# Gate columns of two chunks as one 2x2 block product in seven products; conditioning sums in other stages

## The chip, the cores and the metric

One core of one Trainium2 chip. The metric is device time in microseconds of one execution of the program, inputs in HBM to outputs in HBM; the median of three runs is given.

## What is computed

Two layers of a gated trunk, for 640 tokens: 512 latent tokens and 128 context tokens, with the same weights and separate conditioning. Cut to what matters:

```python
# per layer; x (640, 1024)
shift, scale, gate = split(silu(cond) @ w_mod[l] + b_mod[l], 3)
h = layernorm(x) * (1 + scale) + shift
q, k, v, z_a, cb, cc, cx, z_b, fx, z_c, g = split(h @ w_in[l])      # g: 3 x 1024 columns
y_a = attention(q, k, v) * silu(z_a)
y_b = cb * dwconv3(cc * cx) * silu(z_b)
y_c = real_dft2(fx) * silu(z_c)
gates = sigmoid(g.reshape(-1, 3, 1024))
merged = sum(gates[:, b] * (y[b] @ w_branch[l][b]) for b in range(3))
x = layernorm(alpha * x + gate * (merged @ w_o[l])) * ln_g[l] + ln_b[l]
```

## The kernel before

Activations lie transposed, channels on the partitions. `act` (line 115) is [128, 5 token tiles, 2, 8, 128]: 1024 channels as 8 blocks k of 128, 640 tokens, and each number as a high and a low part in the reduced format fp32r (`split`, line 80: ScalarE copies to the short format, VectorE subtracts to get the rest). A product of two such numbers takes three matmuls: high x high, low x high, high x low.

`inproj` (466) computes one chunk of 128 columns of h @ w_in for all tokens. Its weights are two units of 4 k-blocks, 128x512 (256 KB) each. `product` (457) runs over k and over two token groups of 256 and 384 columns, three matmuls each, into a two-bank PSUM tile from a pool of two (`pm`). `branch` (478) does the same with 4 k-blocks and the transposed branch outputs yb, yc or ya as the moving operand.

Of the 58 chunks of w_in, 24 are gate columns (`C_G` on). In the merge (lines 887 to 904) each chunk of branches 1 (yb) and 2 (yc) is followed by the branch product of the same output columns; for branch 0 (ya) all eight gate chunks come first and then all eight products. `use_g` (829) takes the sigmoid out of PSUM on ScalarE; `use_p` (840) multiplies by it out of PSUM and adds to `mg` on VectorE, and splits the finished sum into `act`, from which the output projection reads.

```python
for k in range(nk):
    for t0, t1, a, b in GROUPS:                      # columns 256:512 and 512:896
        mh, ml = moving(k, 0, t0, t1), moving(k, 1, t0, t1)
        nc.tensor.matmul(ps[:, a:b], lhsT=ld.w(0, k), rhs=mh, ...)
        nc.tensor.matmul(ps[:, a:b], lhsT=ld.w(0, k), rhs=ml, ...)
        nc.tensor.matmul(ps[:, a:b], lhsT=ld.w(1, k), rhs=mh, ...)
```

**Order of the work.** The program is a list of jobs in a fixed order (`run`, 163). Weight loads are issued ahead on the SP queue through a ring of `N_RAW` = 4 raw tiles, and split through a ring of `N_HL` = 5 tiles. Within this, a scheduler (`schedule_with_timeline_sim`, 1114) sets each engine's order of instructions when the program is built; it prefers what stands earlier in the list. On the chip each engine takes its own list in that order, and waits. Large tiles live in storage tags A to F and act, one buffer each; a tile of the same tag gets the buffer only when every reader and writer of the earlier tile is done. Before the change A holds Q, then yc, then the gates `ga` of branch 0; B holds K and V, then mg; C ya; D yb; E the softmax tile P, then the DFT matrix; F the gates of ya.

**Conditioning.** `w_mod` is 6 groups of 512 columns per layer; of the 12 the first four are done at the start on TensorE. The other eight are done on VectorE as sums over 8 k-blocks with a scalar per partition (`mod_add`, 198: lines 201 and 204), followed by a transpose, a reduction and one small matmul (`mod_sum`, 207). All eight groups are 32 pieces of two k-blocks, which the merge of layer 0 puts between its chunks (`piece`, 883).

**Other stages.** Attention (584 to 730) is ten units of a token tile and a key head per layer, scores two units ahead of values, with input products (`fills`) between them. The Fourier part (733 to 875) follows with four groups of channels, then the merge, then the output projection (943), whose `load_wo` (857) splits four large tiles of w_o into tags E, D, F and A.

Of the kernel before, what the change touches and what calls it, by code (L numbers as in the profile page):

```python
# [9 lines left out]
F32 = mybir.dt.float32  # L10
# [8 lines left out]
NT = 5  # L19
# [4 lines left out]
N_RAW = 4  # L24
# [10 lines left out]
def body(nc, tc, I, O, ctx):  # L35
# [8 lines left out]
    tq = pool("tq", 3)  # L44
# [80 lines left out]
    class Unit:  # L125
        def __init__(self, src, nm, plain):
            self.src, self.nm, self.plain = src, nm, plain
            self.read = self.used = False
            self.stage = build_stage[0]

        def dma(self):
            self.raw = wr.tile([128, 512], F32, name=f"raw{self.nm}", tag="raw")
            nc.sync.dma_start(out=self.raw, in_=self.src)

        def split(self, eng):
            self.hl = wp.tile([128, 2, 512], F32R, name=f"hl{self.nm}", tag="hl")
            copy(self.hl[:, 0], self.raw)
            eng.tensor_tensor(out=self.hl[:, 1], in0=self.raw, in1=fr(self.hl[:, 0]), op=ALU.subtract)  # L138
            self.read = True

    class Load:
        def __init__(self, src, n, nm, plain=False):
            self.units = [Unit(src[:, i * 512:(i + 1) * 512], f"{nm}_{i}", plain) for i in range(n)]

        def raw(self, i):
            return self.units[i].raw

        def w(self, z, k):
            return self.units[k // 4].hl[:, z, (k % 4) * 128:(k % 4 + 1) * 128]

# [12 lines left out]
    def run():  # L163
        units = [u for ld, _ in jobs if ld for u in ld.units]
        parts = [u for u in units if not u.plain]
        loaded = halved = 0
        for i, (ld, bd) in enumerate(jobs):
            while i >= 3:
                if (loaded < len(units) and units[loaded].stage <= stage[0]
                        and (loaded < N_RAW or i > 3 and units[loaded - N_RAW].read)):  # L170
                    units[loaded].dma()
                    loaded += 1
                elif (halved < len(parts) and hasattr(parts[halved], "raw")
                      and (halved < N_HL or parts[halved - N_HL].used)):
                    behind = () if halved == 4 or halved > 7 else ("xT",) if halved < 4 else ("hi", "lo")
                    with ExitStack() as st:
                        for name in behind:
                            st.enter_context(tc.issue_after(last[name].ins))
                        parts[halved].split(nc.gpsimd if halved < 4 or parts[halved].nm in POOL_UNITS else nc.vector)
                    halved += 1  # L180
                else:
                    break
            if ld:
                bd(ld)
                for u in ld.units:
                    u.read = u.used = True
# [35 lines left out]

    mod_raw = {}
# [242 lines left out]
    def inproj(l, c, use):  # L466
        ld = Load(I["w_in"][l, c], 2, f"w{l}_{c}")
# [10 lines left out]
    def branch(l, b, c, y, use):  # L478
        def body(ld):
            use(product(mmt(f"pb{l}_{b}_{c}"), ld, 4, lambda k, i, t0, t1: y()[:, k, i, t0 * 128:t1 * 128]))  # L480
        job(body, Load(I["w_branch"][l, b, c], 1, f"b{l}_{b}_{c}"))
# [7 lines left out]
    def layer(l):  # L489
        S = {}  # L490

# [10 lines left out]
        def begin():  # L502
# [14 lines left out]
            S["P"] = big.tile([128, 2, 4, 512], F32, name=f"P{l}", tag="E")  # L517
# [202 lines left out]

        job(scores(0))
# [107 lines left out]
        def use_g(b, c):  # L829
            def use(ps):  # L830
                if b == 0:
                    if c == 0:
                        S["ga"] = big.tile([128, NK, TOK], F32, name=f"ga{l}", tag="A")
                    nc.scalar.activation(S["ga"][:, c], ps, AF.Sigmoid)
                else:
                    S["sg"] = row(f"gs{l}{b}{c}")
                    nc.scalar.activation(S["sg"][:, :TOK], ps, AF.Sigmoid)  # L837
            return use

        def use_p(b, c):  # L840
            def use(ps):
                if b == 1 and c == 0:
                    S["mg"] = big.tile([128, NK, TOK], F32, name=f"mg{l}", tag="B")
                mg = S["mg"][:, c]
                if b == 1:
                    mul(mg, ps, S["sg"][:, :TOK])
                    return
                sg = S["sg"][:, :TOK] if b == 2 else S["ga"][:, c]
# [8 lines left out]
        def load_wo(i, tg, q):  # L857
            def body(ld):
                if q == 0:
                    flat = tg in "EF"  # L860
# [5 lines left out]
            job(body, Load(I["w_o"][l, i // 2, (i % 2) * 2 + q], 2, f"o{l}{i}{q}", True))  # L866

        inproj(l, C_FX, use_fx(0))
        inproj(l, C_FX + 1, use_fx(1))
        for g in range(4):  # L870
            job(channels(g))
            inproj(l, C_ZC + g, use_zc(g))
            job(positions(g))
# [252 lines left out]
```

## Time and profile before

| | |
|---|---|
| median of three runs | 1288.0 us (1287.6 to 1288.98) |
| profiled execution, span | 1287.4 us |
| TensorE busy | 1262.0 us, 8304 matmuls |
| VectorE, ScalarE, GpSimd busy | 779.7, 497.4, 172.4 us |
| HBM read | 124.19 MB |

The profile is one execution; its span runs from the first to the last instruction, and the median of the runs is 0.6 us above it. PE is TensorE's matmuls, PEld its weight loads, DVE VectorE, ACT ScalarE, POOL GpSimd and SP the queue that issues most loads. Matmuls are pipelined: one shows a duration longer than the distance to the next, so the distance between starts is what one costs.

### The profile page before, as it was taken

Reading aid. Unit: us, or ns where it says so; the run is one execution under the profiler, and the core shown is the slowest. Engines: PE = TensorE matmul, PEld = TensorE weight load, DVE = VectorE, ACT = ScalarE, POOL = GpSimd, SP = SyncE. Lnnn points to the kernel's source line nnn. Section 1 sums busy time; section 2 is a strip of 40 time slices with the busy share of each in tenths; the row PEclk is TensorE's granted clock in tenths of the full one; section 3 lists DMA queues with packets and bytes.
Section 4 is the critical chain, followed back from the end, with each engine's and each line's share of the span. In section 5 each row is a group of like instructions: output and inputs, shape, how many; then the busy total and the mean of one; then the engine's idle time right before and its main releaser. Section 6 shows DMA issues by size and latency. Waiting matters only on the chain.

```text
span 1287.4 us, 20922 instructions
## 1 busy us (share of the span) xinstructions
PE 1262.0 (98%) x8304; PEld 1218.7 (95%) x8304; DVE 779.7 (61%) x1418; ACT 497.4 (39%) x929; POOL 172.4 (13%) x164
## 2 busy tenths in 40 slices
PE   5999999999999999999999999999999999999997
PEld 3799999999999999999789999999999999999986
DVE  6785566664599999326887665666455323321576
ACT  5546556543432322222345646555344222222210
POOL 3303323210000000000230234232000000000001
PEclk9999999999999999999999999999999999999999
DMA  9322111131265655221612111113113223222141
GB/s 379 98 78 67 65 51 58 58 115 59 75 223 180 211 179 174 74 74 54 233 71 78 64 61 58 50 58 114 68 56 117 91 91 91 74 75 74 50 180 49
DMA packets 58761, 131.07 MB, mean 102 GB/s; under 512 B 6888, under 2 KB 7464, under 8 KB 58408
## 3 DMA queue, kind: packets, MB, share of 16 engines
q1 hardware_dynamic: 57504, 125.35, 29.2%
q0 software_dynamic: 720, 4.10, 0.9%
q8 instruction: 65, 1.06, 0.4%
q10 hardware_dynamic: 440, 0.30, 0.1%
q14 instruction: 32, 0.26, 0.1%
HBM read 124.19 MB, written 5.52 MB: 101 GB/s over the span
## 4 chain that ended last, share of the span: by engine, by line
PE 95%; DVE 3%; issue 1%; DMA 0%; POOL 0%; ACT 0%; SPq 0%; DVEq 0%; POOLq 0%; ACTq 0%
PE p L461 21%; PE p L463 21%; PE p L462 20%; PE pb L461 4%; PE pb L463 4%; PE pb L462 4%; PE o L951 3%; PE o L950 3%; PE o L949 3%; PE pt L647 2%; PE s L598 2%; PE p L347 2%; PE po L652 1%; PE po L653 1%; PE modp L407 1%
## 5 line engine op out<-in xcount | busy, mean ns | idle before, releaser
L461 PE MATMUL p<-act,hlw 128*128 128x256 f32 (+1 forms) x1792 | 562.4, 314 | 0.9 <-ACT vt L69 0.9
L463 PE MATMUL p<-act,hlw 128*128 128x256 f32 (+1 forms) x1792 | 556.3, 310 | 0.0
L462 PE MATMUL p<-act,hlw 128*128 128x256 f32 (+1 forms) x1792 | 554.6, 309 | 0.0
L461 PEld LDWEIGHTS p<-act,hlw 128*128 128x128 f32 x1792 | 338.4, 189 | 2.9 <-ACT vt L69 1.2
L462 PEld LDWEIGHTS p<-act,hlw 128*128 128x128 f32 x1792 | 337.2, 188 | 1.3
L463 PEld LDWEIGHTS p<-act,hlw 128*128 128x128 f32 x1792 | 337.4, 188 | 1.0
L138 DVE TENSOR_TENSOR hlw<-raww,hlw 128x512 fp32r<-128x512 f32 x226 | 159.2, 706 | 188.1 <-ACT hlw L69 185.3
L69 ACT ACTIVATE hlw<-raww 128x512 fp32r<-128x512 f32 x232 | 145.3, 629 | 247.8 <-PE p L463 163.9
L629 POOL TENSOR_SCALAR P<-P,rc 128x384 f32<-128x384 f32 (+2 forms) x80 | 111.9, 1413 | 232.8 <-ACT hlw L69 103.0
L204 DVE SCALAR_TENSOR_TENSOR moda<-rawm,scond,moda 128x512 f32<-128x512 f32 x112 | 79.2, 748 | 2.3 <-DMA rawm<-in_w_mod 2.2
L138 DVE TENSOR_TENSOR hlb<-rawb,hlb 128x512 fp32r<-128x512 f32 x48 | 33.1, 689 | 57.3 <-ACT hlb L69 57.2
L69 ACT ACTIVATE hlb<-rawb 128x512 fp32r<-128x512 f32 x48 | 30.3, 632 | 87.1 <-PE p L463 79.8
L950 PE MATMUL o<-wo,act 128*128 128x512 f32 (+1 forms) x168 | 63.7, 379 | 0.0
L949 PE MATMUL o<-wo,act 128*128 128x512 f32 (+1 forms) x168 | 63.7, 381 | 0.0
L951 PE MATMUL o<-wo,act 128*128 128x512 f32 (+1 forms) x168 | 62.9, 379 | 0.0
L257 POOL TENSOR_TENSOR rso<-rso,nhalf 128x1 f32<-128x1 f32 x10 | 13.7, 1374 | 334.0 <-DVE rso L256 334.0
L837 ACT ACTIVATE gs<-p 128x640 f32<-128x640 f32 x32 | 22.6, 705 | 91.0 <-PE p L463 91.0
L72 DVE TENSOR_TENSOR pT<-pt,pT 128x512 fp32r<-128x512 f32 x60 | 40.0, 688 | 23.2 <-ACT pT L69 23.1
L138 POOL TENSOR_TENSOR hlw<-raww,hlw 128x512 fp32r<-128x512 f32 x6 | 9.4, 1586 | 294.0 <-DVE mvo L254 288.4
L69 ACT ACTIVATE pT<-pt 128x512 fp32r<-128x512 f32 x60 | 35.0, 594 | 34.8 <-PE pt L647 26.5
L601 DVE CUSTOM_DVE_ANT_0 P<-s,mask 128x384 f32<-128x384 f32 (+1 forms) x64 | 38.6, 620 | 8.4 <-PE s L598 8.2
L623 ACT ACTIVATE P<-P,nm 128x384 f32<-128x384 f32 (+1 forms) x64 | 42.1, 658 | 1.8 <-DVE es L72 1.4
(221 smaller groups left out, 1909.6 us busy)
## 6 DMA issues: line engine op xcount, KB each, us to landing
raww<-in_w_in SPq DMA_DIRECT2D x232, 256.0 KB, 2.7
rawm<-in_w_mod SPq DMA_DIRECT2D x48, 512.0 KB, 4.3
rawb<-in_w_branch SPq DMA_DIRECT2D x48, 256.0 KB, 2.7
rawo<-in_w_o SPq DMA_DIRECT2D x32, 256.0 KB, 2.7
dft<-in_dft POOLq DMA_DIRECT2D x2, 1542.0 KB, 8.4
x<-in_x SPq DMA_DIRECT2D x5, 512.0 KB, 6.0
xr<-in_x SPq DMA_DIRECT2D x5, 512.0 KB, 8.4
xs<-xr SPq DMA_DIRECT2D x5, 512.0 KB, 2.9
```

Of the source, the lines that this page charges most:

```text
L69: nc.scalar.activation(out, in_, AF.Copy)
L72: nc.vector.tensor_tensor(out=out, in0=a, in1=b, op=ALU.subtract)
L138: eng.tensor_tensor(out=self.hl[:, 1], in0=self.raw, in1=fr(self.hl[:, 0]), op=ALU.subtract)
L204: nc.vector.scalar_tensor_tensor(out=acc[:, c], in0=w, scalar=scond[:, k, c:c + 1], in1=acc[:, c], op0=ALU.mult, op1=ALU.add)
L461: nc.tensor.matmul(ps[:, a:b], lhsT=ld.w(0, k), rhs=mh, start=k == 0, stop=False)
L462: nc.tensor.matmul(ps[:, a:b], lhsT=ld.w(0, k), rhs=ml, start=False, stop=False)
L463: nc.tensor.matmul(ps[:, a:b], lhsT=ld.w(1, k), rhs=mh, start=False, stop=k == nk - 1)
L623: nc.scalar.activation(P[:, g, :W], srcs[g], AF.Exp, scale=0.125, bias=nm_[:, g:g + 1], accum_out=sm[:, g:g + 1])
L629: nc.gpsimd.tensor_scalar(out=P[:, g, :W], in0=P[:, g, :W], scalar1=rc[:, g:g + 1], scalar2=None, op0=ALU.mult)
L949: nc.tensor.matmul(ps, lhsT=act[:, t, 0, k], rhs=w[:, 0], start=k == 0, stop=False)
L950: nc.tensor.matmul(ps, lhsT=act[:, t, 0, k], rhs=w[:, 1], start=False, stop=False)
L951: nc.tensor.matmul(ps, lhsT=act[:, t, 1, k], rhs=w[:, 0], start=False, stop=k == NK - 1)
```

## The change

Two chunks of gate columns are taken as the rows of a 2x2 block matrix (a11, a12; a21, a22): the chunks m and m+1 down, the two halves of k across. The activations are the other one: the halves of k down, and two halves of the tokens across (the first and the last 64 of each tile of 128, 320 columns each). The four blocks of the result are made from seven products of 4 k-blocks and 320 columns instead of eight (Strassen's scheme). For that VectorE forms four sums of weight tiles per pair, and once per layer four sums of the activations: three in tiles `T` of their own, and the fourth written over a block of `act`. Four of the seven products accumulate in one bank "y", two in "z", one in "x"; copies and additions take the partial sums into the gate tiles between them. The branch products of a pair now stand between the products of the following pair; for branch 0 they still come after all gates, but the first pair of branch 0 holds the last two products of yc.

The conditioning groups are spread: three to the attention stage of layer 0, one to its Fourier stage, two to its merge and two to the merge of layer 1. mg and xr move to tag E, w_o's tiles to D, B, F and A; the ring of raw tiles has 6 buffers, the pool of 643-column rows 5 instead of 3; the ring for descriptors of POOL's loads is set to 2048 bytes. The loading code becomes a list of steps (splits and sums) in place of units.

```diff
-N_RAW = 4
+N_RAW = 6
-    tq = pool("tq", 3)
+    tq = pool("tq", 5)
...
+    class Sum:
+        def __init__(self, out, a, b, frees=()):
+            self.raws, self.frees = [out, a, b], frees
+
+        def emit(self, eng):
+            out, a, b = self.raws
+            sub(out.tile, a.tile, b.tile)
...
+    def mod_steps(groups, acc, raws):
...
+                fetch(i + len(raws()) - 1)
+                mod_add(acc(), k, raws()[i % len(raws())])
+                if k == NK - 1:
+                    mod_sum(l, n, acc())
...
+        side = mod_steps(((0, 4), (0, 5), (1, 0)) if l == 0 else (), lambda: S["moda"], lambda: S["modr"])
...
             job(values(u))
+            beside(1)
             if u + 2 < 10:
                 job(scores(u + 2))
-                fills(2)
+                fills(1)
+                beside(1)
+                fills(1)
+                beside(1)
...
+        def sums(q):
+            def body():
+                def put(i, t):
+                    hi, lo = (S["T"][i][:, z, 2 * q:2 * q + 2].rearrange("p k n -> p (k n)") for z in range(2))
+                    split(hi, lo, t[:, :TOK])
+                a, b, c = row(f"ta{l}{q}"), row(f"tb{l}{q}"), tmp(f"tc{l}{q}")
+                whole(a, 0, q, 1)
+                whole(b, 0, q, 0)
+                whole(c, 1, q, 1)
+                sub(b[:, :TOK], a[:, :TOK], b[:, :TOK])
+                add(a[:, :TOK], c[:, :TOK], a[:, :TOK])
+                add(c[:, :TOK], c[:, :TOK], b[:, :TOK])
+                put(1, c)
+                put(0, b)
+                put(2, a)
+            return body
+
+        def last_sum():
+            for q in range(2):
+                a, b = row(f"td{l}{q}"), row(f"te{l}{q}")
+                whole(a, 1, q, 0)
+                hi, lo = (S["T"][1][:, z, 2 * q:2 * q + 2].rearrange("p k n -> p (k n)") for z in range(2))
+                add(b[:, :TOK], fr(hi), fr(lo))
+                sub(a[:, :TOK], a[:, :TOK], b[:, :TOK])
+                split(block(0, q, 1, 0), block(0, q, 1, 1), as_block(a))
...
+        def pair(b, m, between=()):
...
+            def seventh(bank, moving, first, then):
+                def body(ld):
+                    if first:
+                        ps[bank] = aux(f"{bank}{nm}")
+                    out = ps[bank][:, :320]
+                    for k in range(4):
+                        for i, (z, y) in enumerate(((0, 0), (0, 1), (1, 0))):
+                            nc.tensor.matmul(out, lhsT=ld.w(z, k), rhs=moving(k, y), start=first and k == i == 0,
+                                             stop=k == 3 and i == 2, skip_group_check=True)
+                    then(out.rearrange("p (t i) -> p t i", i=64))
+                return body
+
+            def keep(i, half):
+                def then(out):
+                    if not G:
+                        if b == 0:
+                            if m == 0:
+                                S["ga"] = big.tile([128, NK, TOK], F32, name=f"ga{l}", tag="A")
...
+                    copy(quarter(G[i], half), out)
+                return then
+
+            def plus(i, half):
+                return lambda out: add(quarter(G[i], half), out, quarter(G[i], half))
...
+            def last_y(out):
+                sigmoid(quarter(G[1], 0), out)
+                sigmoid(quarter(G[1], 1), quarter(G[1], 1))
+
+            def last_z(out):
+                plus(0, 1)(out)
+                sigmoid(G[0], G[0])
+
+            def u3(out):
+                keep(1, 1)(out)
+                plus(1, 1)(ps["z"][:, :320].rearrange("p (t i) -> p t i", i=64))
...
+            job(seventh("y", old(0, 0), True, keep(0, 0)), Load([a11, a21, a22, s3, a12], [hl(a11, [], 1)]))
+            job(seventh("x", old(0, 1), True, plus(0, 0)), Load([], [hl(a12, [], 2)]))
+            job(seventh("y", new(1), False, keep(0, 1)),
+                Load([], [Sum(s3, a21, a11), Sum(a21, a21, a22), Sum(a11, a11, a21), hl(a11, [], 6)]))
+            job(seventh("z", new(0), True, lambda out: None), Load([], [hl(a21, [a21], 5)]))
+            job(seventh("y", new(2), False, u3), Load([], [hl(s3, [s3], 7)]))
+            if between:
+                between[0]()
+            job(seventh("y", lambda k, z: act[:, :, z, k, 64:128], False, last_y), Load([], [hl(a22, [a22], 4)]))
+            job(seventh("z", old(1, 1), False, last_z), Load([], [Sum(a12, a12, a11, [a11]), hl(a12, [a12], 3)]))
+            if between:
+                between[1]()
...
-        for b, y in ((1, "yb"), (2, "yc")):
-            for c in range(NK):
-                inproj(l, C_G + b * 8 + c, use_g(b, c))
-                branch(l, b, c, lambda y=y: S[y], use_p(b, c))
+        before = None
+        for b, y in ((1, "yb"), (2, "yc"), (0, "ya")):
+            for m in range(4):
+                def product_of(i, b_m=before):
+                    b, m, y = b_m
+                    branch(l, b, 2 * m + i, lambda: S[y], use_p(b, 2 * m + i))
+                pair(b, m, [lambda i=i, f=product_of: f(i) for i in range(2)] if before else ())
+                before = (b, m, y) if b else None
                 piece()
...
+                if b == 2 and 1 <= m < 3:
+                    load_wo(0, "D", m - 1)
-        for c in range(NK):
-            inproj(l, C_G + c, use_g(0, c))
-            piece()
         for c in range(NK):
             branch(l, 0, c, lambda: S["ya"], use_p(0, c))
+            if c < 4:
+                load_wo(*((1, "B", 0), (1, "B", 1), (2, "F", 0), (2, "F", 1))[c])
         load_wo(3, "A", 0)
         load_wo(3, "A", 1)
...
-    nc = bacc.Bacc("TRN2", target_bir_lowering=False, num_devices=1)
+    nc = bacc.Bacc("TRN2", target_bir_lowering=False, num_devices=1, dynamic_dma_scratch_size=2048)
```

## Rows read from the trace of the kernel before

**Rows 1.** The page: busy time, share of the span and instructions.
```profile
span 1287.4 us, 20922 instructions
...
PE 1262.0 (98%) x8304; PEld 1218.7 (95%) x8304; DVE 779.7 (61%) x1418; ACT 497.4 (39%) x929; POOL 172.4 (13%) x164
```

**Rows 2.** The chain of work that ended last, by engine.
```profile
PE 95%; DVE 3%; issue 1%; DMA 0%; POOL 0%; ACT 0%; SPq 0%; DVEq 0%; POOLq 0%; ACTq 0%
```

**Rows 3.** Windows: attention 0, Fourier 0, merge 0, part of it, Fourier 1, merge 1.
```profile
core 0: us, PE busy (x) PEld busy (x) DVE busy (x) ACT busy (x) POOL busy (x), PEclk, DMA share, GB/s
62.00:282.00 220.00, 219.15 (x1463) 214.13 (x1463) 142.49 (x302) 118.77 (x238) 58.01 (x51) 1.00 0.21 70
282.00:353.00 71.00, 71.00 (x497) 69.89 (x496) 34.66 (x67) 27.81 (x56) 3.29 (x8) 1.00 0.21 68
353.00:601.00 248.00, 248.00 (x1678) 247.52 (x1678) 187.60 (x303) 66.84 (x109) 0.00 (x0) 1.00 0.47 150
425.00:440.00 15.00, 15.00 (x103) 15.00 (x103) 14.90 (x26) 4.28 (x7) 0.00 (x0) 1.00 0.59 187
916.00:990.00 74.00, 74.00 (x515) 72.81 (x515) 37.61 (x71) 28.82 (x57) 1.55 (x4) 1.00 0.23 73
990.00:1232.00 242.00, 242.00 (x1623) 240.72 (x1622) 84.22 (x119) 64.17 (x104) 0.00 (x0) 1.00 0.26 82
```

**Rows 4.** Timeline of PE: start us, us, engine, line, operation; an input and a branch product.
```profile
401.52 0.28 PE L461 MATMUL p<-act,hlw 128*128 128x256 f32 x1
...
402.41 0.28 PE L461 MATMUL p<-act,hlw 128*128 128x256 f32 x1
...
1000.50 0.28 PE L461 MATMUL pb<-yb,hlb 128*128 128x256 f32 x1
...
1000.86 0.34 PE L461 MATMUL pb<-yb,hlb 128*128 128x384 f32 x1
...
1001.38 0.28 PE L461 MATMUL p<-act,hlw 128*128 128x256 f32 x1
```

**Rows 5.** The same view in the output projection of layer 0.
```profile
608.66 0.39 PE L950 MATMUL o<-wo,act 128*128 128x512 f32 x1
608.89 0.39 PE L951 MATMUL o<-wo,act 128*128 128x512 f32 x1
```

**Rows 6.** Groups of instructions: count, busy us, mean ns of one, idle before.
```profile
L138 DVE TENSOR_TENSOR hlw<-raww,hlw 128x512 fp32r<-128x512 f32 x226 | 159.2, 706 | 188.1 <-ACT hlw L69 185.3 <-PE p L463 1.7
L69 ACT ACTIVATE hlw<-raww 128x512 fp32r<-128x512 f32 x232 | 145.3, 629 | 247.8 <-PE p L463 163.9 <-PE pb L463 64.6 <-DMA raww<-in_w_in 13.0
L204 DVE SCALAR_TENSOR_TENSOR moda<-rawm,scond,moda 128x512 f32<-128x512 f32 x112 | 79.2, 748 | 2.3 <-DMA rawm<-in_w_mod 2.2
...
L75 DVE TENSOR_TENSOR ga<-pb,ga 128x640 f32<-128x640 f32 x16 | 13.2, 824 | 11.3 <-PE pb L463 11.3
...
L209 DVE STREAM_TRANSPOSE modf<-moda 128x1024 f32<-128x1024 f32 x8 | 9.9, 1239 | 0.0
L211 DVE TENSOR_REDUCE modg<-modf 128x32 f32<-128x1024 f32 x8 | 9.7, 1214 | 0.1
...
L72 DVE TENSOR_TENSOR al<-f,ah 128x384 fp32r<-128x384 f32 x8 | 4.4, 551 | 0.1
...
L69 ACT ACTIVATE ah<-f 128x384 fp32r<-128x384 f32 x8 | 3.9, 492 | 0.3
L78 DVE TENSOR_TENSOR ff<-fx 128x255 f32<-128x255 f32 x8 | 3.4, 425 | 11.1 <-PE f L766 7.1 <-ACT fx L69 3.9
...
L69 ACT ACTIVATE fy<-g 128x257 f32<-128x257 f32 x8 | 3.1, 382 | 5.7 <-PE f L766 5.7
```

**Rows 7.** DMA issues: KB each, median us from issue to landing.
```profile
raww<-in_w_in SPq DMA_DIRECT2D x232, 256.0 KB, 2.7
```

**Rows 8.** Timeline of all engines where a matmul waits for ScalarE's copy.
```profile
62.10 0.70 ACT L69 ACTIVATE vt<-p 128x640 f32<-128x640 f32 x1 [0.32 <-PE p L347]
...
62.86 0.39 PE L461 MATMUL p<-act,hlw 128*128 128x256 f32 x1 [0.85 <-ACT vt L69]
```

More of the change, by code (lines that the diff above doesn't have):

```diff
@@ L122, in scale, with __init__, load @@
         return modT[:, l, 2 * j + 1, s:s + 1]
[L125 to L128, printed above, removed]
+    class Raw:
+        def __init__(self, src, nm):
+            self.src, self.nm, self.tile = src, nm, None
             self.stage = build_stage[0]
[L131 to L135, printed above, removed]
-            self.hl = wp.tile([128, 2, 512], F32R, name=f"hl{self.nm}", tag="hl")
-            copy(self.hl[:, 0], self.raw)
-            eng.tensor_tensor(out=self.hl[:, 1], in0=self.raw, in1=fr(self.hl[:, 0]), op=ALU.subtract)
-            self.read = True
+        def load(self):
+            self.tile = wr.tile([128, 512], F32, name=f"raw{self.nm}", tag="raw")
+            if self.src is not None:
+                nc.sync.dma_start(out=self.tile, in_=self.src)
@@ L141, in body, with __init__, load @@
     class Load:
-        def __init__(self, src, n, nm, plain=False):
-            self.units = [Unit(src[:, i * 512:(i + 1) * 512], f"{nm}_{i}", plain) for i in range(n)]
+        def __init__(self, raws, steps=(), frees=()):
+            self.raws, self.steps, self.frees = raws, steps, frees
+            self.units = [s for s in steps if isinstance(s, Split)]
         def raw(self, i):
-            return self.units[i].raw
+            return self.raws[i].tile
         def w(self, z, k):
             return self.units[k // 4].hl[:, z, (k % 4) * 128:(k % 4 + 1) * 128]
+    def load(src, n, nm, plain=False):
+        raws = [Raw(src[:, i * 512:(i + 1) * 512], f"{nm}_{i}") for i in range(n)]
+        if plain:
+            return Load(raws, frees=raws)
+        return Load(raws, [Split(r, r.nm, [r]) for r in raws])
@@ L178, in run @@
                             st.enter_context(tc.issue_after(last[name].ins))
-                        parts[halved].split(nc.gpsimd if halved < 4 or parts[halved].nm in POOL_UNITS else nc.vector)
-                    halved += 1
+                        x.emit(nc.gpsimd if split < 4 or x.nm in POOL_UNITS else nc.vector)
+                    split += 1
+                    hl_live += 1
                 else:
                     break
+                raw_live -= len(x.frees)
+                done += 1
             if ld:
+                assert all(hasattr(u, "hl") for u in ld.units) and all(r.tile is not None for r in ld.raws), i
                 bd(ld)
-                for u in ld.units:
-                    u.read = u.used = True
+                hl_live -= len(ld.units)
+                raw_live -= len(ld.frees)
             else:
@@ L719, in fills, with beside @@
                     inproj(l, *fill.pop(0))
+        side = mod_steps(((0, 4), (0, 5), (1, 0)) if l == 0 else (), lambda: S["moda"], lambda: S["modr"])
+        def beside(n):
+            for _ in range(n):
+                if side:
+                    job(side.pop(0))
         job(scores(0))
```

141 lines of the change are left out of this document (101 added, 40 removed).

## The prediction

> **What bounds the kernel now.** I read the page's busy times first: TensorE 1262.0 of 1287.4 us, VectorE 779.7, ScalarE 497.4 [rows 1]. A busy TensorE may still wait inside its pipeline, so the chain of waits came next: 95% of the chain that ended last is TensorE, VectorE has 3% [rows 2]. Then the windows by stage [rows 3]: in both Fourier stages (71 and 74 us) and in both gate and merge stages (248 and 242 us) TensorE is busy for the whole stretch, and the granted clock is 1.00, the upper of its two levels (2.4 GHz). VectorE's share differs a lot: 187.60 of 248 us in the gates of layer 0, where it also does the conditioning sums, but 84.22 of 242 us in layer 1. In one stretch of 15 us VectorE was busy for 14.90 us and TensorE still did not stop. So the time of a gate stage is its number of matmuls times their spacing, as long as the helpers keep up. Durations below are of this execution: span 1287.4 us, against a median of 1288.0 us of three runs; I add 0.6 us at the end. A measurement of this kernel can tell some 0.2% (2.6 us) from no change.
>
> **Spacing of a matmul.** In a branch product six matmuls (three of 256 columns, three of 384) go from 1000.50 to 1001.38, 0.88 us; in an input product from 401.52 to 402.41, 0.89 us [rows 4]. That is 0.1475 us for a mean of 320 columns; the three of 256 take 0.12 each, the three of 384 0.17, and one of 512 takes 0.23 [rows 4, 5]. Cost follows the columns, so 320 columns at once should cost 0.1475 us too; the interpolation leaves 0.145 to 0.150. The new moving operand is five runs of 64 columns. The two rows of six compare whole contiguous runs with runs of 128: 0.88 and 0.89 us. I take the shorter runs at nothing, with twice the difference of the two rows as the upper bound, 0.02/6 = 0.003 us per matmul; 4 of 7 products read such runs in place, 1152 matmuls, so at most 4 us.
>
> **What goes away.** Before, a pair of gate chunks is 2 chunks x 8 k x 2 groups x 3 = 96 matmuls. After, 7 products x 4 k x 3 = 84. With 12 pairs in each of 2 layers 24 x 12 = 288 matmuls go: 288 x 0.1475 = **42.5 us**, all of it on TensorE's path. The Trainium skill, in "TensorE: Matmul & The Clock Gate", Back-to-back issue gap, gives N/2.4 + 2.5 ns, so 0.136 us for 320 columns: by that 39 us would go. The rows, at 0.147, decide.
>
> **What is added beside TensorE.** A VectorE subtraction of 128x512 is 0.706 us, ScalarE's copy of that size 0.629; 255 and 384 columns take VectorE 0.425 and 0.551 (so 0.48 for 320), and ScalarE needs 0.382 and 0.492 for 257 and 384 (so 0.44) [rows 6]. Per pair VectorE gets three more weight splits (2.1), four weight sums (2.8) and three additions out of PSUM (1.45): 6.4 us, 76 us per layer. ScalarE gets three more weight copies (1.9), three copies out of PSUM (1.3) and a little more sigmoid (0.2): 41 us per layer. In layer 1 VectorE then has 84 + 76 + two groups of conditioning sums. A group costs (79.2 + 9.9 + 9.7)/8 = 12.4 us [rows 6]: 185 us, in 242 - 21 = 221 us. In layer 0 six of eight groups leave the stage: 188 + 76 - 74 = 190 of 227 us. ScalarE has some 105 of 221. That fits under TensorE on average, and the 14.90 of 15 us above say that a nearly full VectorE need not stop it: I cost it at nothing. If the cover is gone, the stage lasts as long as VectorE's list.
> DMA traffic of the weights stays the same; a load of 256 KB lands 2.7 us after its issue [rows 7], and with six raw tiles and five split ones the loads run several products ahead. The conditioning fetches stand in the same SP queue and wait for a tile that VectorE frees; the weight loads behind them wait with them, hidden by the same lead. The smaller descriptor ring touches only loads on POOL's queue: nothing, at worst a late DFT table and 5 us per layer.
>
> **What it gives back, on the path.**
> *The y bank.* Four of seven products accumulate into one PSUM bank, and ScalarE reads the partial sum out three times in between, so product 3 waits for the copy after product 1, 5 for 3, 6 for 5. What this costs uncovered is in the trace once: a copy of 640 columns starts at 62.10, takes 0.70 us, and the next matmul starts at 62.86, 0.06 after it; TensorE idled 0.85 us [rows 8]. With 0.44 for the copy that is 0.6 us of idling. Normally x, z or a branch product lies between (12 matmuls, 1.77 us, or 24, 3.54 us), against a chain of some 0.6 us, or 1.2 us behind one weight copy. I take 0.07 us for each of 24 x 3 handovers (nearest: the windows of the same stages, no idle time at all; other end 0.6): **5 us**. Product 7 waits in the same way for VectorE's addition out of z; the three pairs of branch 0 without products between, and the first pair, are in this term.
> *Pair (0,0).* Its first copy opens the gate tile in storage A, where yc lies, while the last two yc products are put between the products of that very pair. The buffer passes on only after yc's last reader, so these two go ahead of product 3. The second needs the fifth split tile, and waits until the first has freed it: a copy and a subtraction, 0.63 + 0.71, with handovers some 1.6 us; then the copy is uncovered, 0.6 to 0.9. I take 2.5 us per layer (0 if something fills it, 5 if nothing does): **5 us**.
> *Fourier of layer 0.* VectorE has 34.66 of 71 us; one group of sums (12.4) and 26 operations of 640 columns for the activations' sums (0.824 each alone [rows 6], 21.4) make 68.5, without the first pair's weight sums. Nothing is spare, product 3 of the first pair may be late: 0 to 5, I take **2 us**. In layer 1, 37.61 + 21.4 = 59 of 74 us: nothing.
> *Branch 0 at the end.* Two w_o tiles can be split only after the last pair. 8 x (3 x 0.82 + 0.71) + 12 x 0.7 = 34 us of VectorE stand against 8 x 3.54 = 28 us of products; half tiles of the output projection follow that need only the early chunks. 0 to 5 per layer, I take 1: **2 us**.
> *Attention of layer 0.* Three groups, 37 us, join 142.49 of 220: 82%. POOL and the softmax chain have a lead of two units. Nothing; the rival below prices the other end.
> Sum: 1287.4 - 42.5 + 5 + 5 + 2 + 2 = 1258.9 of span, and 0.6: **1259.5 us**; I say 1259.
>
> **Rivals.**
> *Nearly all of it stays* (1246 to 1252): every give-back is covered, as nearly all waits of the old stages are: TensorE is busy for 248.00 of 248 us. 1288 - 42.5 = 1245.5. For: the order of instructions is planned with the waits known. Against: pair (0,0) has no cover in the code.
> *VectorE gets in the way* (1268 to 1285): 24 conditioning steps of about 1.5 us now stand between softmax steps in layer 0. If each keeps the transposes waiting for half of its time, 18 us come back, 1277. For: attention has a chain over four engines. Against: 18% of VectorE stays free there, and the old gate stage bore the same steps at 76% busy.
> *The bank's handovers are bare* (about 1300, slower): ScalarE takes its list in order. If a weight copy in front waits for a late weight sum of VectorE, the copy out of y waits behind it, and TensorE with it. At 0.6 to 0.9 us, say 0.77, for 72 handovers it costs 55 us: 1287.4 - 42.5 + 55 + 0.6 = 1300. It decides from 42.5/72 = 0.59 us per handover on, when ScalarE is later than its cover of 1.77 us by that much. For it: VectorE at over 80%, a chain weight sum to split to matmul in three steps. Against: ScalarE is half idle, the loads lead by several products.
> The Trainium skill, in "Perfetto Trace Analysis", Matmuls, asks for independent groups to rotate through banks so that the evacuation of one lies beside the matmuls of the next; this change returns to one bank four times per pair, so by that rule the last rival is the danger. The row at 62.86 agrees that an uncovered evacuation stops TensorE; no row of before shows a covered one of this kind.
> That the products are fewer can be counted in the code, so "it does nothing" is no case by itself.
>
> **How the numbers follow.** Forecast (give-backs of 8 to 24 us) 0.50; nearly all stays 0.22; VectorE in the way 0.15; gain and loss cancel within 2.6 us 0.03; slower 0.10. Faster by over 0.2%: 0.50 + 0.22 + 0.15 = 0.87. The range from 1245 (the full gain) to 1280 (most of the third case) leaves out about 0.18. The bound of 4 us on the short runs lies within it.
>
> **What would show it.** Right: 8304 - 288 = 8016 matmuls; 0.147 us between matmuls of 320 columns; some 227 and 221 us for the two gate stages, nearly without idling but for a gap of 2 to 3 us where branch 2 passes to branch 0; VectorE at 80 to 85% there. Wrong: spacing over 0.152; TensorE idling before the product after each copy out of y, with ScalarE as releaser; idling in layer 0's attention with VectorE as releaser.

## The result and the profile after

The median is 1267.9 us (1267.4 to 1271.0) against 1288.1 (1287.6 to 1289.0) for the kernel before on the same chip: ratio 0.9845 [0.9831, 0.9859], 20 us faster. The forecast was 1259. The page of after, with the answers to [rows 1] and [rows 2]:

```profile
span 1266.1 us, 20852 instructions
...
PE 1226.5 (97%) x8016; PEld 1178.1 (93%) x8016; DVE 950.4 (75%) x1710; ACT 577.5 (46%) x1113; POOL 174.1 (14%) x164
...
PE 91%; DVE 3%; DMA 3%; issue 1%; ACT 1%; POOL 0%; DVEq 0%; SPq 0%; POOLq 0%; ACTq 0%
```

There are 8304 - 288 = 8016 matmuls, as counted. TensorE is busy 35.5 us less, yet the span fell by only 21.3, so some 14 us of new idling lie between. Windows of after, with the columns of [rows 3]: the steady pairs of layer 0, the passage from branch 2 to branch 0, the same two of layer 1, then the end of the Fourier stage with the first pair, in layer 0 and in layer 1.

```profile
378.00:516.00 138.00, 138.00 (x940) 137.80 (x941) 107.57 (x177) 58.04 (x111) 0.00 (x0) 1.00 0.35 111
516.00:530.00 14.00, 12.45 (x81) 11.55 (x80) 9.34 (x14) 3.86 (x8) 0.00 (x0) 1.00 0.14 44
...
976.00:1080.00 104.00, 104.00 (x711) 104.00 (x710) 86.94 (x141) 45.73 (x87) 0.00 (x0) 1.00 0.36 115
1120.00:1135.00 15.00, 13.46 (x87) 12.55 (x87) 9.10 (x14) 3.97 (x8) 0.00 (x0) 1.00 0.24 74
...
347.00:352.00 5.00, 2.16 (x10) 1.51 (x8) 4.90 (x10) 2.21 (x5) 0.00 (x0) 0.76 0.15 52
352.00:354.00 2.00, 1.66 (x6) 1.43 (x6) 2.00 (x5) 0.72 (x1) 0.00 (x0) 0.50 0.00 0
...
962.00:968.00 6.00, 0.95 (x6) 0.68 (x5) 6.00 (x9) 3.56 (x7) 0.00 (x0) 0.95 0.61 211
968.00:976.00 8.00, 6.35 (x32) 5.86 (x33) 8.00 (x16) 2.65 (x5) 0.00 (x0) 0.83 0.00 1
```

In the Fourier and merge stages four stretches lose time and no others: 138.00 of 138 and 104.00 of 104 us of steady pairs are busy. The large losses stand at 347 to 362 and 962 to 976, where the first Strassen pair begins beside the last Fourier products. There VectorE is full and the granted clock falls to 0.50, the lower level (1.2 GHz). What TensorE waited for, over the span (us in total, times, longest); of the rows shown all but the first are new:

```profile
PE tr L333 <- DVE xn L322: 10.2, 3, 9.1
PE z L964 <- ACT fy L69: 6.3, 2, 5.1
...
PE y L964 <- ACT gs L69: 2.1, 2, 1.6
PE g L869 <- DVE al L72: 2.1, 1, 2.1
PE pb L516 <- ACT hlb L69: 1.9, 3, 0.7
PE g L871 <- DVE al L78: 1.1, 1, 1.1
PE y L964 <- ACT ga L69: 1.1, 2, 0.5
```

The timeline at the end of the Fourier stage of layer 0. `al` is the remainder in the split of the last group's channels; `tb` and `sgzc` are 640-column operations of the activations' sums and of yc.

```profile
347.20 0.82 DVE L78 TENSOR_TENSOR tb<-act 128x640 f32<-128x640 f32 x1
...
348.74 0.68 DVE L143 TENSOR_TENSOR hlg010p<-rawg010s,hlg010p 128x512 fp32r<-128x512 f32 x1
349.34 0.42 DVE L72 TENSOR_TENSOR al<-f,ah 128x256 fp32r<-128x256 f32 x1
349.81 0.58 PE L869 MATMUL g<-dft,ah 128*128 128x256 f32 x1 [2.09 <-DVE al L72]
350.41 0.82 DVE L75 TENSOR_TENSOR sgzc<-p,sgzc 128x640 f32<-128x640 f32 x1
351.14 0.81 DVE L72 TENSOR_TENSOR tb<-ta,tb 128x640 f32<-128x640 f32 x1
351.87 0.61 DVE L78 TENSOR_TENSOR al<-al,f 128x256 fp32r<-128x256 f32 x2
352.34 0.58 PE L871 MATMUL g<-dft,al 128*128 128x258 f32 x1 [1.10 <-DVE al L78]
```

A sum (`tb`) and a split of gate weights stand in VectorE's list ahead of `al`, for which the Fourier products wait. In layer 1 the same crowd shows up on ScalarE:

```profile
960.71 1.97 PE L964 MATMUL x<-act,hlg110p 128*128 128x320 f32 x12
964.71 0.82 DVE L78 TENSOR_TENSOR tc<-tc,tb 128x640 f32<-128x640 f32 x1
965.56 0.74 ACT L69 ACTIVATE tb<-tc 128x640 fp32r<-128x640 f32 x1 [1.57 <-DVE tc L78]
966.29 0.74 ACT L69 ACTIVATE act<-td 128x640 fp32r<-128x640 f32 x1
967.03 0.66 ACT L69 ACTIVATE fy<-g 128x257 f32<-128x257 f32 x2
967.74 2.50 PE L964 MATMUL z<-tb,hlg110p 128*128 128x320 f32 x8 [5.05 <-ACT fy L69]
```

The product of the first pair that comes third in time (`z`, the fourth in the code's list) reads the sum `tb` and wants a PSUM buffer that `g` holds until ScalarE has copied it to `fy`. Two copies of sums (into `tb` and `act`) stand ahead of `fy` in ScalarE's list, and the first waits for VectorE's `tc`. TensorE idles 5.05 us.

To find where time is lost I cut the span at four matmuls that every version has: the first Fourier product of each layer and the last product with ya of each. Taking 288/2 matmuls x 0.1475 = 21.2 us from before gives the full gain: 296.9 and 295.0 us for the two middle stages.

| us | start | layer 0, Fourier to ya | between | layer 1, the same | end |
|---|---|---|---|---|---|
| before | 289.7 | 318.1 | 303.4 | 316.2 | 60.0 |
| after | 291.0 | 308.8 | 301.0 | 305.0 | 60.3 |
| full gain | | 296.9 | | 295.0 | |

So 12 and 10 us did not arrive. The start varies between 291.0 and 295.5 us over the profiles below, even where nothing in it was edited, so the experiments are read by the two middle stages first and by the total second. What varies is the clock: in the two profiles with 291.0 us (after and, below, "earlier and prepared") the granted clock is 1.00 from 16 us to the end of the start. In the eight others that keep conditioning groups in the attention stage it is 0.50 for 6.8 to 13.7 us of the start, and in each of them it falls between 60.0 and 62.4 us. One window of after and the same of a longer start (293.2 us, "gates in rows"):

```profile
62.00:69.00 7.00, 6.15 (x42) 5.83 (x41) 7.00 (x14) 2.65 (x5) 0.00 (x0) 1.00 0.67 199
62.00:69.00 7.00, 6.15 (x24) 5.64 (x23) 6.99 (x13) 1.86 (x4) 0.00 (x0) 0.51 0.70 211
```

### The profile page after: what moved, and what is told of

It reads as the page before. It is cut to its first block, busy times and chain, and to the rows that moved or that the text cites. A ratio compares the mean times of both kernels' runs of the same rounds, so it can differ in the third digit from the quotient of the medians.

```text
span 1266.1 us, 20852 instructions
## 1 busy us (share of the span) xinstructions
PE 1226.5 (97%) x8016; PEld 1178.1 (93%) x8016; DVE 950.4 (75%) x1710; ACT 577.5 (46%) x1113; POOL 174.1 (14%) x164
## 4 chain that ended last, share of the span: by engine, by line
PE 91%; DVE 3%; DMA 3%; issue 1%; ACT 1%; POOL 0%; DVEq 0%; SPq 0%; POOLq 0%; ACTq 0%
PE y L964 13%; PE p L516 12%; PE p L518 12%; PE p L517 12%; PE z L964 6%; PE pb L516 5%; PE pb L518 5%; PE pb L517 4%; PE x L964 3%; PE o L1142 3%; PE o L1140 3%; PE o L1141 3%; PE pt L705 2%; PE s L656 2%; DMA rawm<-in_w_mod 1%; DMA raww<-in_w_in 1%
## 5 line engine op out<-in xcount | busy, mean ns | idle before, releaser
L516 PE MATMUL p<-act,hlw 128*128 128x256 f32 (+1 forms) x1024 | 321.2, 314 | 0.9 <-ACT vt L69 0.9
L518 PE MATMUL p<-act,hlw 128*128 128x256 f32 (+1 forms) x1024 | 318.4, 311 | 0.0
L517 PE MATMUL p<-act,hlw 128*128 128x256 f32 (+1 forms) x1024 | 317.4, 310 | 0.0
L516 PEld LDWEIGHTS p<-act,hlw 128*128 128x128 f32 x1024 | 193.4, 189 | 2.6 <-ACT vt L69 1.2
L517 PEld LDWEIGHTS p<-act,hlw 128*128 128x128 f32 x1024 | 192.7, 188 | 1.3
L518 PEld LDWEIGHTS p<-act,hlw 128*128 128x128 f32 x1024 | 192.7, 188 | 1.2
L69 ACT ACTIVATE hlw<-raww 128x512 fp32r<-128x512 f32 x136 | 84.8, 629 | 114.8 <-PE p L518 103.2
L143 DVE TENSOR_TENSOR hlw<-raww,hlw 128x512 fp32r<-128x512 f32 x130 | 91.3, 704 | 22.8 <-ACT hlw L69 21.1
L69 ACT ACTIVATE gs<-y 128x320 f32<-128x320 f32 x48 | 20.9, 435 | 68.8 <-PE y L964 65.1
L72 DVE TENSOR_TENSOR rawg<-rawg,rawg 128x512 f32<-128x512 f32 x72 | 49.5, 687 | 1.2
L516 PE MATMUL pb<-yc,hlb 128*128 128x256 f32 (+1 forms) x128 | 40.1, 313 | 1.4 <-ACT hlb L69 1.4
L516 PE MATMUL pb<-yb,hlb 128*128 128x256 f32 (+1 forms) x128 | 40.0, 313 | 0.5 <-ACT hlb L69 0.5
```

The lines of the kernel that those rows point to most:

```text
L69: nc.scalar.activation(out, in_, AF.Copy)
L72: nc.vector.tensor_tensor(out=out, in0=a, in1=b, op=ALU.subtract)
L143: eng.tensor_tensor(out=self.hl[:, 1], in0=raw, in1=fr(self.hl[:, 0]), op=ALU.subtract)
L516: nc.tensor.matmul(ps[:, a:b], lhsT=ld.w(0, k), rhs=mh, start=k == 0, stop=False)
L517: nc.tensor.matmul(ps[:, a:b], lhsT=ld.w(0, k), rhs=ml, start=False, stop=False)
L518: nc.tensor.matmul(ps[:, a:b], lhsT=ld.w(1, k), rhs=mh, start=False, stop=k == nk - 1)
```

## The experiments

Theory A: the arithmetic of the activations' sums crowds VectorE at the border of Fourier stage and merge, and the pauses there are what is missing. Rivals: the bare handovers of bank y (B); only the position of the last sum in the list (C); the conditioning group that layer 0's Fourier stage took on (D).

**Sums left out, first try.** `T` is filled with plain copies by GpSimd and the fourth block isn't written, so the sums' arithmetic is left out.

```diff
-                a, b, c = row(f"ta{l}{q}"), row(f"tb{l}{q}"), tmp(f"tc{l}{q}")
...
-                put(2, a)
+                for i in range(3):
+                    for z in range(2):
+                        nc.gpsimd.tensor_copy(out=S["T"][i][:, z, 2 * q:2 * q + 2]..., in_=block(i % 2, q, i // 2, z))
...
-            if g == 3:
-                job(last_sum)
```

> Leaves out the arithmetic of the activations' sums: the tiles T get copies of blocks of act from GpSimd, and the fourth block of act is not overwritten, so the seven products run on other numbers and the output is not the reference's. Theory A (volume: the 26 VectorE and 16 ScalarE instructions of the sums per layer, bunched at the end of the Fourier stage, hold TensorE up, and the lower clock follows from that pause): the 12.1 and 9.0 us of excess between 340 and 378 us and between 957 and 984 us go, 1246 to 1250 us. Theory B (the first pair has its own slow start: four weight sums and no branch product between): at least half of it stays, 1257 us or more.

1262.4 us, 0.9794 [0.9776, 0.9812]. (The sums have 8 ScalarE instructions per layer; the 16 of the expectation are those of both layers.) Layer 0 took 306.2 us; layer 1 took 291.7, but the part between was 8.7 us longer. The run does not decide: GpSimd also assembles the Fourier input, and with the copies ahead of it TensorE now waits there (`f`, 5.2 us). At the borders themselves the waits on `al` and `fy` were gone, so I repeated it without GpSimd.

**The same, clean.** Products 3 to 5 read blocks of `act` in place; the sums are gone with nothing in their stead.

```diff
             def new(i):
-                return lambda k, z: S["T"][i][:, z, k]
+                return old(i % 2, i // 2)
...
-                job(begin_sums)
-                job(sums(0))
...
-                job(last_sum)
```

> Leaves out the activations' sums altogether, and nothing stands in their place on any engine: products 3 to 5 read blocks of act, and the fourth block is not overwritten, so the output is not the reference's. The run before with copies on GpSimd had a new pause in the Fourier stage, behind those copies. Theory A (volume of the sums): only the first pairs' own 2.5 us per layer stay of 12.0 and 9.0 us, and nothing new comes in the Fourier stage: 1250 to 1254 us. Theory B (the first pair is slow by itself): 1258 us or more.

1255.2 us, 0.9734 [0.9719, 0.9749], 1.2 us above theory A's range and below B's; 299.2 and 298.7 us: 9.6 and 6.3 of the 12 and 10 us come back, and the clock stays at 1.00 in both borders. The waits of `g` for `al` and of `z` for `fy` are gone from the list; it now has these at the first pair, on a weight split:

```profile
PE y L964 <- DVE hlg011p L143: 1.3, 1, 1.3
PE y L964 <- DVE hlg111p L143: 1.3, 1, 1.3
```

A holds: without the sums most of the loss is gone. The next runs ask whether it is their volume or their place.

**The last sum moved back**, behind the loop over groups.

```diff
-            if g == 3:
-                job(last_sum)
             beside(1)
...
+        job(last_sum)
         pieces = [...]
```

> Only the place of the fourth sum in the list of jobs changes: behind the last group of the Fourier stage instead of ahead of its second half. Theory A (volume): the same work is bunched, 1264 to 1270 us. Theory C (order: the copies out of the Fourier stage's last PSUM banks stand in ScalarE's list behind splits that wait for VectorE, so bank z of the first pair is late): the wait of 5.05 us for fy in layer 1 and that of some 1.4 us in layer 0 go, with the clock's drop in layer 1: 1257 to 1261 us.

1270.4 us, 0.9849 [0.9833, 0.9866]; 307.9 and 305.4, so nothing gained. The wait of `z` for `fy` went, and others took its place:

```profile
PE y L964 <- ACT gs L69: 3.1, 4, 1.7
PE y L964 <- DVE hlg111p L143: 2.7, 1, 2.7
PE g L869 <- DVE al L72: 2.1, 1, 2.1
```

C falls: while VectorE is full, a new order only chooses which item is late.

**One conditioning group moved** from the Fourier stage of layer 0 to its merge.

```diff
-        if l == 0:
-            side.extend(mod_steps(((1, 1),), lambda: fm["a"], lambda: fm["r"]))
-            job(begin_mod)
...
-        pieces = [... ((2, 3) if l == 0 else (4, 5)) ...]
+        pieces = [... ((1, 2, 3) if l == 0 else (4, 5)) ...]
```

> Only conditioning group (1,1) goes from the Fourier stage of layer 0 to the merge; the sums stay where the change has them. Theory A (the length of VectorE's list at the end of that stage, whatever it is made of): in layer 0 the stretch from the first Fourier product to the last product of ya (308.8 us) loses 4 to 9 us, layer 1 (305.0 us) stays within 1 us; 1259 to 1264 us. Rival (it is the sums' own chain and place): both stay within 1.5 us, 1266 to 1269 us.

1267.6 us, 0.9839 [0.9824, 0.9854], against after the same within the runs; but layer 0 fell from 308.8 to 305.4 us, and layer 1 stayed (305.3). The total does not show it, since the start was 2.5 us longer in this profile. The waits on `al` are gone and both layers now show the same one:

```profile
PE z L964 <- ACT fy L69: 10.1, 2, 5.1
```

So D explains 3.4 us of layer 0, just less than the 4 I had as the low end, and the total was missed (1259 to 1264); the rest is common to both layers.

**Sums earlier.** The first pair of sums comes at the start of the Fourier stage, the second after group 0; the group of the run before moved as well.

```diff
-            job(begin_mod)
+        job(begin_sums)
         inproj(l, C_FX, use_fx(0))
+        job(sums(0))
...
-            if g == 1:
-                beside(99)
-                job(begin_sums)
-                job(sums(0))
-            if g == 2:
+            if g == 0:
                 job(sums(1))
```

> The first three sums start at the beginning of the Fourier stage, and conditioning group (1,1) moves from the Fourier stage of layer 0 to the merge. The volume is the same, but spread over 60 us; the fourth sum stays where it is. Theory A (volume bunched at the end): 1250 to 1256 us. Theory C (order of the fourth sum and the last copies): mostly unchanged in layer 1, 1260 to 1266 us.

1259.5 us, 0.9771 [0.9753, 0.9788]; 302.4 and 302.0. 6.4 and 3.0 us are back; 3.4 of the 6.4 belong to the group (the run before), so the earlier place is worth 3 us in each layer, with the same arithmetic done. Theory A's 1250 to 1256 us weren't reached, and the next run shows why.

**Sums earlier, and the fourth sum's arithmetic too**: its two rows are computed after group 2, and only the split into `act`, which must wait for the last reader, stays at the end. The conditioning group is moved here too.

```diff
-        def last_sum():
+        def early_sum():
...
+        def last_sum():
+            for q in range(2):
+                split(block(0, q, 1, 0), block(0, q, 1, 1), as_block(S["d", q]))
...
+            if g == 2:
+                job(early_sum)
```

> Early sums and the fourth sum's arithmetic ahead of the last group, but pieces from the first pair on and yc's storage as in the change. If the fourth sum's arithmetic is what the version with early sums still waited for: 1253 to 1256 us, the two stretches of 302.4 and 302.0 us with early sums alone come down to about 300 us. If the conditioning pieces of the first pair are: 1258 to 1260 us, 302 us.

1252.6 us, 0.9731 [0.9714, 0.9747]; 298.7 and 298.5, as short as with no sums at all. What had remained was the fourth sum's arithmetic. So theory A needs the word place for volume: with the same VectorE work earlier in the list the stages are as short as without it.

**Gates of pair (0,0) in rows of their own**, so storage A keeps yc until its last product is done.

```diff
-                            if m == 0:
+                            if m == 1:
                                 S["ga"] = big.tile([128, NK, TOK], F32, name=f"ga{l}", tag="A")
-                            G.extend(S["ga"][:, 2 * m + j] for j in range(2))
+                            G.extend(S["ga"][:, 2 * m + j] if m else row(f"gs{nm}{j}")[:, :TOK] for j in range(2))
```

> The first pair of branch 0 keeps its gates in two row buffers; the tile in storage A is opened one pair later, when yc has been read. Theory (storage: the last two yc products must go ahead of product 3): 2.4 us per layer go, 1263 us. Rival (the pause belongs to the passage from branch 2 to branch 0, or to the ring of five split tiles): 1267 to 1268 us.

1266.8 us, 0.9826 [0.9811, 0.9841]: only 1.1 below after. The pauses where branch 2 passes to branch 0 are gone (2.4 us per layer by the distances of matmuls), and the stages are 1.6 and 1.7 us shorter (a pause of 0.4 us in the next pair is new); the start was 2.2 us longer in this profile, by the lower clock shown above, so the total hid it. In after that passage reads:

```profile
519.26 0.63 ACT L69 ACTIVATE hlb<-rawb 128x512 fp32r<-128x512 f32 x1 [2.90 <-PE pb L518]
519.95 0.38 PE L516 MATMUL pb<-yc,hlb 128*128 128x256 f32 x1 [0.72 <-ACT hlb L69]
520.74 0.39 PE L518 MATMUL pb<-yc,hlb 128*128 128x256 f32 x1 [0.30 <-DVE hlb L143]
524.35 0.44 ACT L69 ACTIVATE ga<-y 128x320 f32<-128x320 f32 x1 [4.46 <-PE pb L518]
524.84 2.02 PE L964 MATMUL y<-tb,hlg000p 128*128 128x320 f32 x12 [0.53 <-ACT ga L69]
```

The split for yc's second product comes late, then the copy out of y is bare: the order and the sizes the prediction gave.

**Every copy out of y made twice**, against B.

```diff
                     copy(quarter(G[i], half), out)
+                    copy(quarter(G[i], half), out)
```

> Each of the three copies out of bank y per pair is made twice: 72 more ScalarE copies of 0.44 us, each on the way to the next product of that bank. If the handovers are covered (x, z or a branch product between): 1268 to 1273 us, and no excess in the steady pairs. If they are at the edge of their cover, as the slower rival of the prediction had it: up to 72 x 0.44 = 32 us more, 1290 to 1300 us.

1273.0 us, 0.9877 [0.9862, 0.9892]. The steady pairs of layer 0 have one stop of 0.63 us and no other:

```profile
385.00:516.00 131.00, 130.37 (x888) 130.09 (x887) 102.48 (x168) 60.24 (x123) 0.00 (x0) 1.00 0.33 108
```

That stop, at 425.93 us, is for a split of branch weights that comes late on ScalarE; the scheduler planned this version anew, and the branch product stands at another place there than in after. The stages are 1.7 and 1.2 us longer: about 0.5 us in each at the passage from branch 2 to branch 0, where the bare handover grows from 0.53 to 1.05 us, and the rest at that stop and at the first pairs. Most of the remaining difference to after is the start, 4.5 us longer in this profile. B falls: 72 more copies cost 3 us, not 32, so even twice the copy, 0.87 us, is covered by the 1.77 us of matmuls between.

**All eight conditioning groups back in the merge of layer 0**, three pieces behind each pair: the change without its second half.

```diff
-        side = mod_steps(((0, 4), (0, 5), (1, 0)) if l == 0 else (), ...)
+        side = mod_steps((), ...)
...
-                piece()
+                for _ in range(3):
+                    piece()
```

> Undoes the spreading: all eight conditioning groups stand in the merge of layer 0 again, three pieces per pair. Theory (VectorE's list there becomes longer than TensorE's: some 180 us and six more groups of 13 us each, 258 us, against 227 us): 20 to 35 us more in that merge, less up to 6 us that the Fourier stage of layer 0 gets back, 1283 to 1297 us. Rival (a nearly full VectorE does not stop TensorE, as before the change): 1262 to 1268 us.

1296.1 us, 1.0049 [1.0032, 1.0066]: 0.5% slower than before. Layer 0 takes 342.0 us, 33 more than after. Its largest waits and a window:

```profile
PE modq L247 <- DVE modg L243: 17.9, 3, 9.5
PE z L964 <- ACT fy L69: 10.1, 2, 5.1
```
```profile
520.00:560.00 40.00, 27.09 (x156) 25.73 (x155) 38.88 (x63) 10.49 (x20) 0.00 (x0) 0.83 0.40 135
```

VectorE is full, and the small matmul `modq` that closes a conditioning group stands in TensorE's list and waits there for VectorE's reduction, with the gate products behind it. The clock falls to 0.50 within the two longer of the three waits (6.67 and 9.45 us), for 10.2 us each. With the groups in this place the change doesn't pay; a finer spreading inside the merge was not tried.

The start is 5 us shorter than in after (285.8 against 291.0), and that is a cost of the spreading. In after the scheduler draws the first conditioning sums (`P<-sz,scond`) ahead, from 52.10 us on, among the VectorE operations that prepare `act` for the first products, and TensorE waits for `act`. Waits between 30 and 75 us, in after and in this run:

```profile
PE p L402 <- DVE act L508: 3.3, 4, 1.4
PE p L402 <- DVE act L508: 0.6, 1, 0.6
```

The 300th matmul starts at 63.9 us in after and at 59.2 us here; from there to the first Fourier product both take 227 us. The kernel before shows 289.7 us although its clock was at 0.50 from 30.1 to 36.9 us, which neither of these two shows, so its 1.3 us less than after understate this cost.

**Everything that helped, together**: both moves of the sums, with the conditioning group, the gates of pair (0,0) in rows, and the conditioning pieces only from the second pair on.

```diff
-                piece()
+                if b == 2 or m:
+                    piece()
+                if l == 0 and b == 2 and m < 2:
+                    piece()
```

> A version that should be faster: the first three sums from the start of the Fourier stage on, the arithmetic of the fourth before the last group (only its split waits), group (1,1) and all conditioning pieces from the second pair on, and the gates of the first pair of branch 0 in row buffers. If the bunched volume and yc's storage are the causes: 8 us as in the run with early sums, 4.8 us at the two pauses of branch 0, 3 to 5 us at the first pairs, 1250 to 1254 us. If the first pairs are late by themselves: 1256 to 1260 us.

1248.9 us, 0.9688 [0.9674, 0.9703]: faster than both kernels, with the whole computation in it. Windows of the end of the Fourier stage of layer 0 and of layer 1:

```profile
340.00:378.00 38.00, 36.62 (x249) 35.62 (x248) 36.91 (x64) 17.25 (x36) 0.00 (x0) 1.00 0.43 142
950.00:985.00 35.00, 33.62 (x225) 32.70 (x224) 34.46 (x58) 15.55 (x31) 0.00 (x0) 1.00 0.43 149
```

VectorE is as full as in after (36.91 of 38 us, against 36.51 in the same window there); what went is the urgent work behind work that could wait. Against "earlier and prepared" the stages are 1.7 and 2.0 us shorter. The gates in rows had given 1.6 and 1.7 by themselves, so the later start of the conditioning pieces is worth 0.3 us at most. All by stages:

| us | median | layer 0 | layer 1 |
|---|---|---|---|
| after | 1267.9 | 308.8 | 305.0 |
| last sum moved back | 1270.4 | 307.9 | 305.4 |
| group to merge | 1267.6 | 305.4 | 305.3 |
| gates in rows | 1266.8 | 307.2 | 303.3 |
| copies twice | 1273.0 | 310.5 | 306.2 |
| sums earlier | 1259.5 | 302.4 | 302.0 |
| no sums, clean | 1255.2 | 299.2 | 298.7 |
| earlier and prepared | 1252.6 | 298.7 | 298.5 |
| together | 1248.9 | 297.0 | 296.5 |
| full gain | | 296.9 | 295.0 |

## Why the prediction was right, and where not

*The removal* was right: 288 matmuls fewer, and 940 starts in 138.00 us are 0.1468 us each, with moving runs of 64 columns in place. The short runs cost nothing: in the steady pairs of both layers the products that read `act` so are 0.1465 us apart from start to start, those that read whole runs of `T` 0.1467. The Trainium skill's N/2.4 + 2.5 ns ("TensorE: Matmul & The Clock Gate", Back-to-back issue gap), which that section gives for an isolated matmul, would make it 0.136, an estimate; the trace does not agree.

The added operations had the sizes that the interpolation gave (0.44 and 0.48 us for 320 columns, 0.71 for a weight sum); groups of after, columns as [rows 6]:

```profile
L69 ACT ACTIVATE gs<-y 128x320 f32<-128x320 f32 x48 | 20.9, 435 | 68.8 <-PE y L964 65.1
L72 DVE TENSOR_TENSOR rawg<-rawg,rawg 128x512 f32<-128x512 f32 x72 | 49.5, 687 | 1.2
```

*The y bank* (5 us) was too much: between 378 and 516 us there is no idling at all, and doubling the copies adds one stop of 0.63 us. The rival with bare handovers is wrong where other products lie between; where they do not, one handover cost 0.53 us with a copy of 0.44, as [rows 8] had it. The Trainium skill's advice to rotate independent groups through banks ("Perfetto Trace Analysis", Matmuls) decides nothing here: the runs show that returning to one bank is free with 12 matmuls in between (138.00 of 138 us busy).

*Pair (0,0)* (2.5 us per layer) measured 2.4, by the named mechanism, and went when the storage was separated. *Attention* was put at nothing, and at 18 us by the second rival. From 104 to 282 us TensorE is busy for 178.00 of 178 us with VectorE at 132.88, so between the softmax steps the conditioning costs nothing and the rival's reason is wrong. But the first steps are drawn ahead into the start, where they cost some 5 us (63.9 against 59.2 us at the 300th matmul), and the eight profiles in which the lower clock follows have a start that is 1.3 to 4.5 us longer still. The sum had no such term. *Branch 0 at the end* (2 us): no pause was found there. *Layer border*: the part between the two middle stages is 2.4 us shorter, which no step of the prediction had.

*The Fourier stages* are the step that failed: "Nothing is spare, product 3 of the first pair may be late: 0 to 5, I take 2 us. In layer 1, 37.61 + 21.4 = 59 of 74 us: nothing." The first pair was nearly the right place (in layer 0 the last Fourier products wait too), but the pauses and slow matmuls at the border (the distances between starts beyond the usual one of each width, added up) come to 12.1 us in layer 0 and 9.0 in layer 1; by the same count the kernel before has 1.4 us at each border. The mistake was to spread VectorE's work over the stage. Two windows of after, first and last part of layer 1's stage:

```profile
901.00:947.00 46.00, 46.00 (x322) 45.17 (x321) 29.73 (x56) 18.55 (x38) 2.44 (x6) 1.00 0.14 42
947.00:976.00 29.00, 22.30 (x144) 21.27 (x144) 28.16 (x49) 13.74 (x27) 0.00 (x0) 0.94 0.23 73
```

The code places the sums behind groups 1, 2 and 3, so for 46 us VectorE has a third of its time free, and then it is full for 29 us in which the Fourier copies, the first weight sums and `T` are all wanted. The 14.90 busy of 15 us in [rows 3], which I read as a licence, came from a stretch of conditioning sums that no product waited for.

A second part was not in the sum: the clock. The granted clock was 0.50 from 349.6 us, near the end of the pause of 2.09 us, to 359.8, with the pause of 1.10 us in between; in layer 1 it was 0.50 from 967.4 us, near the end of the pause of 5.05 us, to 970.8. The first product of the pair, in the timeline of after:

```profile
354.22 3.57 PE L964 MATMUL y<-act,hlg010p 128*128 128x320 f32 x12
357.59 0.41 PE L871 MATMUL g<-dft,al 128*128 128x256 f32 x1
```

Twelve matmuls start from 354.22 to 357.59, 0.28 us apart on average (the first 0.43, the others 0.267), in place of 0.147. Without the pauses 8.9 us of work ran like this in layer 0 (the 10.2 less 0.2 and 1.1), and 3.1 us in layer 1 (967.74 to 970.8); at 0.147/0.267 that is 4.0 and 1.4 us lost, an estimate from these rows. The rest, 8.1 and 7.6 of the 12.1 and 9.0 us, is waiting. That neither border of the runs "together" and "no sums, clean" shows the lower clock fits it, but the clock was not tried by itself (such as with idle matmuls to fill the pauses), so its share stays an estimate.

*The total* came nearer than its terms. The give-backs were put at 14 us, and 21 came (42.5 less the 21.3 by which the span fell). The Fourier borders cost some 21 us where 2 stood; that the total was missed by only 9 us is in part luck, since the 7 us put at the y bank and at the end of branch 0 were not spent and the layer border gave 2.4. The measured 1267.9 lies at the edge of the second rival (1268 to 1285): VectorE was in the way, as that rival had it, but in the start and at the Fourier borders and not between the softmax steps.

## What to carry to other kernels

A helper engine's load must be read window by window at the border where its results are wanted: a forecast mean of 80% over the stage hid 29 us at 97%. When a transformation needs derived operands, compute them as soon as their inputs exist and leave only what a reader forbids for the end; here that, with three smaller moves, was worth 19 us at the same arithmetic. Work that is moved into another stage may be drawn further ahead by the scheduler than it was put: look at the start of that stage as well. A copy out of PSUM between two uses of one bank was free here wherever other products longer than it lay between.

## What was not expected of the hardware

A pause of a few microseconds can cost more than itself, by the lower clock that stood behind the two above. The length of the low stretch did not follow the length of the pause: 10.2 us with pauses of 2.09 and 1.10, but 3.4 with one of 5.05. Nor did the same pauses always bring it: between 53 and 61 us after, "earlier and prepared" and "gates in rows" have four pauses each of nearly the same lengths (0.99, 0.23, 1.15 and 1.45 us in after), and only in the third did the clock fall behind them, from 62.0 to 68.8 us. And a bare handover of a bank adds only 0.1 us to the copy: 0.53 us of idling for a copy of 0.44.
